# Modulation in three norms and on VectorE; one visit per step in two attentions

## The chip, the cores and the metric

One core of a Trainium2 chip runs the whole program. Its engines work side by side, each in its own fixed order: TensorE (PE, with its weight loads as PEld), VectorE (DVE), ScalarE (ACT), GpSimd (POOL) and SyncE (SP); transfers are issued from the queues of SP, ACT and POOL. They wait for one another by semaphores. The metric is the time of one execution on the device in microseconds (us), as the median of a few runs.

## The reference

The program is a stack for 512 latent tokens of width 1024. The first block has two layers with modulation: a vector per layer, from the condition `c` (and `c_ctx` for the 256 context tokens), gives shift, scale and gate of the mixer's norm and of the FFN's norm.

```python
mod = silu(c) @ ada_w[i] + ada_b[i]            # 6 x 1024 numbers per layer
sh1, s1, g1, sh2, s2, g2 = split(mod, 6)
h = rms_norm(x, norm1_g[i]) * (1 + s1) + sh1
x = x + g1 * mixer(h)                           # layer 0: gated linear attention, layer 1: neighbourhood attention
h = rms_norm(x, norm2_g[i]) * (1 + s2) + sh2
x = x + g2 * conv_ffn(h)
```

The second block has two layers, each with multi-head latent attention (causal softmax), stick-breaking attention and retention side by side, a gated output and an MLP. All is float32.

## The kernel before

Tokens stand along the free dimension, features along the partitions in `KD` = 8 groups of 128. A float32 product is made of three products of split operands: `mm3` (lines 327 to 334) multiplies high by high, low by high and high by low part; `weight()` (L311) loads a weight tile from SP's queue, ScalarE makes its high part (L319) and VectorE the low part (L320). In names, `hh` and `hl` (later `xh`, `xl`) are the halves of a normed input, `whi` and `wlo` those of a weight.

The modulation is cut into sections `sg` of 2048 numbers: section 0 for the first norm, then 1 to 5. Each section has two halves of 1024. There are two ways to work one out:

- `gada` on TensorE: 16 steps, a load of 128x1024 (tile `aw`) and two matmuls with `scT` (silu of the condition) as stationary operand, each into one of four groups of 32 columns of one bank (`ad`, L373); then VectorE transposes the bank (L380) and adds the bias. Sections 1 and 2 are worked out so during the GLA block, as filler; section 5 in the two norms around the first FFN, with loads on ScalarE's queue.
- `vada` on VectorE: per half, 16 loads of 128x512 (tile `at`, two buffers), each multiplied by two scalars and added to two sums (`aa`, L406 for the first, L408 for the others); then matmuls with a unit operand (L416) move the sums to the layout. Sections 3 and 4 are worked out so during the first FFN.

Filler is put in by `weave` (L229): a main generator yields how much time its step leaves to other engines, and the filler is advanced until it has yielded as much. `mixed` (L241) puts one step of a side generator into a filler whenever that has yielded `every`; in the GLA block `every` is `AEV` (2.5), and `ada()` (L803) is the side. The program's builder then sets each engine's order by when operands are ready, so an operation that depends on loads alone can stand far ahead of its place in the code; buffers of a pool keep it from running before they are free.

A norm goes in four steps: the squares' sums over the 8 groups (`sumsq`, L479, on VectorE), one product with ones on TensorE (`rstd`, L351), logarithm and exponential on ScalarE (L301), and `modulate`: VectorE (L498), ScalarE (L510, the high half) and VectorE again (L511, the low half). For the very first norm this is `modulate0`: ScalarE (L520), POOL (L521) and VectorE (L524). L576 applies the root there. "Norm 1" below is the one ahead of the first FFN, "norm 2" ahead of the neighbourhood attention, "norm 3" ahead of the second FFN. `block1_out` writes a block's output into the residual: L866 and L869 on VectorE.

The neighbourhood attention (`na`) runs `attend` for pairs of heads: scores of a step (L1004), transposes of the step two back (`trans`, L1027), and every other step the value products of the steps four back (`mix`, L1044), with a yield after each, so that the next heads' projection comes in between. `mla` in the second block does the same (scores, `mla_tr`, `mla_av`, L1426) with stick-breaking and retention as filler.

Of the kernel before, what the change touches and what calls it, by code (L numbers as in the profile page):

```python
# [17 lines left out]
P = 128  # L18
# [3 lines left out]
KD = 8  # L22
# [46 lines left out]
AEV = 2.5  # L69
# [78 lines left out]
def _lay_out(inp):  # L148
# [7 lines left out]
    for l in range(2):  # L156
        w = g["ada_w"][l].reshape(KD, P, 6, KD, 4, 32)
        b = g["ada_b"][l].reshape(6, KD, P)
        for va, vb in ((1, 0), (2, 3), (4, 5)):
# [4 lines left out]
            else:  # L164
                aw.append(s.transpose(0, 1, 4, 2, 3, 5).reshape(KD, P, 2048))
# [92 lines left out]
class Net:  # L258
# [127 lines left out]
    def vada(self, sg, pool):  # L386
        nc, io = self.nc, self.io
        m = self.mod[sg] = self.C.tile([P, 16, 2], F32, name=f"mod{sg}")
        b = self.vec("ada_b", 16 * sg, 16).unsqueeze(2).to_broadcast([P, 16, 2])
        steps = [(half, kc, c) for half in range(2) for kc in range(KD) for c in range(2)]  # L390

        def load(half, kc, c):
            t = self.sb(pool, [P, 512], "at", 2)
            o = 1024 * half + 512 * c
            nc.sync.dma_start(out=t, in_=io["ada_w"][sg - 1, kc, :, o:o + 512])
            return t

        t = load(*steps[0])
        for i, (half, kc, c) in enumerate(steps):
# [10 lines left out]
            yield  # L410
            if kc + c == KD:
                ps, R = self.mm(), slice(64 * half, 64 * half + 64)
# [5 lines left out]
                d = self.sb(pool, [P, NT], "acc", 1)[:, :512]  # L418
                nc.vector.transpose(out=d[R], in_=ps[R])
                nc.vector.tensor_tensor(out=m[R], in0=d[R].rearrange("p (j r) -> p j r", r=32)[:, :, 0:2], in1=b[R],  # L420
                                        op=ALU.add)
                yield
# [59 lines left out]
    def token_rstd(self, pool, x, parts, tags, ps=None):  # L482
# [68 lines left out]
    def gla(self, x, rs, hh, hl, yd, pool, early):  # L551
# [321 lines left out]
    def ffn(self, l, x, hh, hl, sg, pool, parts, tcv, tyh, tyl, side=iter(())):  # L873
# [4 lines left out]
        def proj(piece):  # L878
# [6 lines left out]
            next(side, None)  # L885
            next(side, None)
# [25 lines left out]
    def na(self, hh, hl, yh, yl, pool):  # L912
# [943 lines left out]
```

## Time and profile before

| | |
|---|---|
| median of three executions | 3698.85 us (3698.39 to 3700.05) |
| profiled execution | 3697.38 us, span 3695.6 us |
| PE busy | 3617.4 us, 98% of the span |
| VectorE busy | 2175.7 us, 59% |
| ScalarE busy | 1434.2 us, 39% |
| POOL busy | 361.7 us, 10% |
| mean TensorE clock granted | 0.994 |
| mean DMA rate | 97 GB/s |

A page of the profile names each group of instructions by line, engine and tile, with busy time, mean duration of one and the idle time before it. A busy PE isn't PE at its peak: records of matmuls overlap, and the time from one start to the next tells what one costs. Lines are those of the kernel before.

### The profile page before, as it was taken

The page shows a single profiled execution, that of the slowest core. Times are in us where ns is not written, and L with a number is a line of the kernel's source. Part 1 is how long each engine was busy: PE and PEld are TensorE (multiplying, and loading weights), DVE is VectorE, ACT ScalarE, POOL GpSimd, SP SyncE. Part 2 cuts the span into 40 slices and gives each one's busy share as a digit, 9 for nine tenths or more (in the row PEclk, how much of TensorE's full clock was granted, in tenths as well). Part 3 has the DMA queues.
Part 4 walks back from the last instruction along what each step waited for, and adds up shares of the span by engine and source line. Part 5 has one row for each costly group of instructions (what it writes and reads, how often), then busy time and mean ns, then how long its engine had stood idle before and what let it go on. Part 6 is the DMA issues. An engine that isn't in the chain of part 4 may idle for free.

```text
span 3695.6 us, 48674 instructions
## 1 busy us (share of the span) xinstructions
PE 3617.4 (98%) x19296; PEld 2972.7 (80%) x19296; DVE 2175.7 (59%) x3471; ACT 1434.2 (39%) x2199; POOL 361.7 (10%) x342
## 2 busy tenths in 40 slices
PE   7999999999999998999999999999999999999998
PEld 5778878888878886888787877888888787788888
DVE  5566776364355776444766775544456687644446
ACT  4334432121344454333546534422234653432223
POOL 2000000000001110000210121210121012121011
PEclk9999999999999999999999999999999999999999
DMA  6332343232112222323322232323332223233323
GB/s 254 123 95 66 120 151 107 71 117 83 60 62 58 52 57 66 99 95 99 116 82 87 92 102 80 120 97 97 97 119 82 91 89 104 81 120 98 97 94 118
DMA packets 128931, 360.21 MB, mean 97 GB/s; under 512 B 31664, under 2 KB 33968, under 8 KB 128704
## 3 DMA queue, kind: packets, MB, share of 16 engines
q1 hardware_dynamic: 97632, 321.70, 27.1%
q10 hardware_dynamic: 28928, 27.47, 2.6%
q0 software_dynamic: 2144, 7.93, 0.6%
q8 instruction: 152, 2.49, 0.3%
q14 instruction: 75, 0.61, 0.1%
HBM read 342.10 MB, written 8.65 MB: 95 GB/s over the span
## 4 chain that ended last, share of the span: by engine, by line
PE 45%; DVE 3%; issue 1%; ACT 1%; POOL 0%; DMA 0%; SPq 0%; DVEq 0%; POOLq 0%; ACTq 0%
PE mm L330 13%; PE mm L334 13%; PE mm L332 13%; PE yp L1335 1%; DVE wlo L320 1%; PE yp L1426 1%; PE mm L1238 1%; PE ma L1495 1%; PE mm L1240 0%; PE mm L1239 0%; PE ma L1414 0%; DMA tf<-s 0%; POOL ta L1483 0%; DVE ta L1478 0%; PE ma L1398 0%
## 5 line engine op out<-in xcount | busy, mean ns | idle before, releaser
L319 ACT ACTIVATE whi<-wst 128x1024 fp32r<-128x1024 f32 (+3 forms) x519 | 544.1, 1049 | 1335.8 <-PE mm L332 1113.5
L320 DVE TENSOR_TENSOR wlo<-wst,whi 128x1024 fp32r<-128x1024 f32 (+3 forms) x519 | 690.0, 1330 | 270.6 <-ACT whi L319 264.8
L330 PE MATMUL mm<-xh,whi 128*128 128x512 f32 x1664 | 664.4, 400 | 6.1 <-DVE ta L1124 3.0
L332 PE MATMUL mm<-xl,whi 128*128 128x512 f32 x1664 | 651.1, 391 | 1.6 <-DVE xl L1153 1.6
L334 PE MATMUL mm<-xh,wlo 128*128 128x512 f32 x1664 | 650.4, 391 | 0.0
L330 PE MATMUL mm<-ty,whi 128*128 128x512 f32 (+1 forms) x1008 | 381.1, 378 | 0.1
L334 PE MATMUL mm<-ty,wlo 128*128 128x512 f32 (+1 forms) x1008 | 378.9, 376 | 0.0
L330 PEld LDWEIGHTS mm<-xh,whi 128*128 128x128 f32 x1664 | 313.5, 188 | 79.7 <-issue 15.4
L334 PEld LDWEIGHTS mm<-xh,wlo 128*128 128x128 f32 x1664 | 313.0, 188 | 69.0 <-issue 2.1
L332 PEld LDWEIGHTS mm<-xl,whi 128*128 128x128 f32 x1664 | 313.6, 188 | 62.6 <-DVE xl L1153 2.0
L330 PE MATMUL mm<-hh,whi 128*128 128x256 f32 (+2 forms) x1176 | 339.6, 352 | 7.7 <-ACT hh L510 2.9
L332 PE MATMUL mm<-hl,whi 128*128 128x256 f32 (+2 forms) x1176 | 333.2, 347 | 0.7 <-DVE hl L524 0.4
L334 PE MATMUL mm<-hh,wlo 128*128 128x256 f32 (+2 forms) x1176 | 331.2, 345 | 1.7 <-DVE wlo L320 1.7
L332 PE MATMUL mm<-ta,whi 128*128 128x512 f32 (+1 forms) x752 | 279.1, 371 | 0.4 <-DVE ta L325 0.4
L330 PEld LDWEIGHTS mm<-hh,whi 128*128 128x128 f32 (+1 forms) x1176 | 189.2, 189 | 56.7 <-issue 21.0
L330 PEld LDWEIGHTS mm<-ty,whi 128*128 128x128 f32 x1008 | 189.7, 188 | 37.6 <-issue 4.2
L334 PEld LDWEIGHTS mm<-ty,wlo 128*128 128x128 f32 x1008 | 189.6, 188 | 37.0 <-issue 2.6
L334 PEld LDWEIGHTS mm<-hh,wlo 128*128 128x128 f32 (+1 forms) x1176 | 189.8, 188 | 31.1 <-DVE wlo L320 2.7
L332 PEld LDWEIGHTS mm<-hl,whi 128*128 128x128 f32 (+1 forms) x1176 | 189.0, 188 | 27.8 <-DVE hl L508 1.8
L332 PEld LDWEIGHTS mm<-ta,whi 128*128 128x128 f32 x752 | 141.7, 188 | 25.1 <-DVE ta L325 0.6
L1681 DVE TENSOR_TENSOR x<-x,mm 128x512 f32<-128x512 f32 x56 | 38.5, 687 | 172.1 <-PE mm L334 172.1
L869 DVE SCALAR_TENSOR_TENSOR x<-mm,mod,x 128x512 f32<-128x512 f32 x52 | 38.9, 749 | 164.7 <-PE mm L334 164.7
(427 smaller groups left out, 5920.4 us busy)
## 6 DMA issues: line engine op xcount, KB each, us to landing
wst<-w_in SPq DMA_DIRECT2D x100, 512.0 KB, 3.4
wst<-ffn_in SPq DMA_DIRECT2D x88, 512.0 KB, 3.4
wst<-w_dn SPq DMA_DIRECT2D x70, 512.0 KB, 3.4
wst<-w_up SPq DMA_DIRECT2D x64, 512.0 KB, 3.4
aw<-ada_w SPq DMA_DIRECT2D x40, 512.0 KB, 5.1
at<-ada_w SPq DMA_DIRECT2D x64, 256.0 KB, 3.2
wst<-w_v SPq DMA_DIRECT2D x32, 512.0 KB, 3.4
wst<-ffn_out SPq DMA_DIRECT2D x32, 448.0 KB, 3.3
```

The lines of the kernel that those rows point to most:

```text
L319: nc.scalar.activation(out=hi[:, :n], in_=st[:, :n], func=AF.Copy)
L320: nc.vector.tensor_tensor(out=lo[:, :n], in0=st[:, :n], in1=hi[:, :n].bitcast(F32), op=ALU.subtract)
L330: nc.tensor.matmul(o, whi, xh, start=first, stop=False)
L332: nc.tensor.matmul(o, whi, xl, start=False, stop=False)
L334: self.after = nc.tensor.matmul(o, wlo, xh, start=False, stop=last)
L869: nc.vector.scalar_tensor_tensor(out=x[:, n, a:b], in0=o[:, :b - a], scalar=gsc, in1=x[:, n, a:b], op0=ALU.mult, op1=ALU.add)
L1238: nc.tensor.matmul(o, a, wh[:, ws], start=(k == 0), stop=False)
L1335: nc.tensor.matmul(yp[64 * e:64 * e + 64, sb * P:], v[h // 4][:, sb, c:c + 64], a, start=(sb == 0), stop=True, skip_group_check=True)
L1426: nc.tensor.matmul(yp[64 * e:64 * e + 64, b * P:b * P + P], vm[p // 2][:, c, c0:c0 + 64], T[:, c * P:c * P + P], start=(c == 0), stop=(c = ...
L1495: nc.tensor.matmul(z[:, (s2 - s) * P:], wt, part, start=False, stop=True, skip_group_check=True)
L1681: nc.vector.tensor_tensor(out=x[:, n, :], in0=x[:, n, :], in1=o, op=ALU.add)
```

## The change

1. In the GLA block the side is now `vada` of the first half of section 2, then `gada(1)`; `gada(2)` is gone. `AEV` goes from 2.5 to 4.4.
2. `vada` takes a list of halves, loads on POOL's queue, ends each half with eight unit matmuls of 256 columns in four groups, and yields 0.
3. `gadah` is new: one half section on TensorE, with matmuls of 256 columns over the four groups. Norm 1 has (2, second half), norm 2 (5, first half), both in 8 steps of 1024 columns with seven `aw` buffers on ScalarE's queue; norm 3 has (5, second half) in 16 steps of 512 columns, with four buffers named `bm` on POOL's queue.
4. The sections from 2 on are laid out in memory by halves.
5. `attend` and `mla` issue value products, transposes and scores of a step in one go and then yield once.

```diff
-AEV = 2.5
+AEV = 4.4
@@ vada
-    def vada(self, sg, pool):
+    def vada(self, pool, parts, dst):
...
-            nc.sync.dma_start(out=t, in_=io["ada_w"][sg - 1, kc, :, o:o + 512])
+            nc.gpsimd.dma_start(out=t, in_=io["ada_w"][sg - 1, kc, :, o:o + 512])
...
-            yield
+            yield 0.0
...
+                ps = self.mm()[:, :256]
                 for r in range(2):
-                    for g in range(2):
-                        o = 64 * half + 32 * g
-                        nc.tensor.matmul(ps[o:o + 32, :], self.unit[:, r, :], acc[r][:, 512 * g:512 * g + 512],
+                    for g in range(4):
+                        nc.tensor.matmul(ps[32 * g:32 * g + 32, :], self.unit[:, r, :], acc[r][:, 256 * g:256 * g + 256],
...
+    def gadah(self, sg, v, width, lag, tile, queue, bank):
+        nc, io = self.nc, self.io
+        steps = [(kc, o) for kc in range(KD) for o in range(0, 1024, width)]
+        st = []
+        for i in range(len(steps) + lag):
+            if i < len(steps):
+                kc, o = steps[i]
+                t = tile()
+                queue.dma_start(out=t, in_=io["ada_w"][sg - 1, kc, :, 1024 * v + o:1024 * v + o + width])
+                st.append(t)
+            if i == lag - 1:
+                yield 0.0
+                ps = bank()[:, :256]
+            if i >= lag:
+                kc, o = steps[i - lag]
+                for c in range(0, width, 256):
+                    g = (o + c) // 256
+                    i2 = nc.tensor.matmul(ps[32 * g:32 * g + 32, :], self.scT[:, kc, :], st[i - lag][:, c:c + 256],
+                                          start=(kc == 0), stop=(kc == KD - 1), skip_group_check=True)
+                    self.order(i2, self.after)
+                yield 0.45
...
+        d = tile()[:, :256]
+        nc.vector.transpose(out=d, in_=ps)
...
@@ token_rstd
         acc = self.sumsq(pool, x, KD, parts, tags)
+        hook()
         rs = self.sb(tags.get("keep", pool), [P, hi], *tags["rs"])
@@ gla
         def ada():
-            for sg in range(1, 3):
-                yield from self.gada(sg, pool, (("aw", AW),), AW - 1)
+            yield from self.vada(pool, ((2, 0),), ("at", 2))
+            yield from self.gada(1, pool, (("aw", AW),), AW - 1)
@@ na
         def attend(p):
             for i in range(8 * p, 8 * p + 8):
-                scores(*steps[i])
-                yield 1.0
+                if i >= 4 and i % 2 == 0:
+                    mix(steps[i - 4][0] // 2, steps[i - 4][1])
                 if i >= 2:
                     trans(*steps[i - 2])
-                    yield 1.0
-                if i >= 4 and i % 2 == 0:
-                    mix(steps[i - 4][0] // 2, steps[i - 4][1])
-                    yield 2.0
+                scores(*steps[i])
+                yield 3.0
@@ mla
+                if i >= 4 and i % 2 == 0:
+                    mla_av(blocks[i - 4][0] // 2, blocks[i - 4][1])
+                if 0 <= i - 2 < n:
+                    mla_tr(*blocks[i - 2])
                 if i < n:
                     mla_scores(*blocks[i])
...
+                yield 3 * FILL[0]
@@ emit
-                ada = net.gada(5, F, (("aw", 7),), 7, nc.scalar)
+                ada = net.gadah(2, 1, 1024, 7, aw, nc.scalar, ad)
...
-                rs = norm(*ADA5[:2])
+                rs = norm(ada, *ADA5[:2])
+                drain(ada)
+                ada = net.gadah(5, 0, 1024, 7, aw, nc.scalar, ad)
+                next(ada)
...
-                        (None for sg in (3, 4) for _ in net.vada(sg, F)))
+                        net.vada(F, ((3, 0), (3, 1), (4, 0), (4, 1)), ("at", 2)))
...
+                    ada = net.gadah(5, 1, 512, 4, half, nc.gpsimd,
+                                    lambda: net.ps.tile([P, 512], F32, tag="sc", bufs=1, name="sc"))
+                    next(ada)
...
-                    rs = net.token_rstd(N, x2, [(0, NL)], dict(acc=("P", 3), rs=("rsb", 1), sq=("T", 4), keep=X))
+                    rs = net.token_rstd(N, x2, [(0, NL)], dict(acc=("P", 3), rs=("rsb", 1), sq=("T", 4), keep=X),
+                                        hook=lambda: [next(ada, None) for _ in range(6)])
+                    drain(ada)
```

The places where the order of instructions differs most, one engine at a time. Line numbers in the rows of after are those of the changed kernel, about 30 higher.

VectorE at the start of the program, before: the seven adds of the first norm's sum of squares (`A`), then the first piece of section 0 (`mod`, `gs`), and the application of the root to `F`.

```order
L1206 TENSOR_TENSOR fgm<-vecs 128x8
L479 TENSOR_TENSOR A<-A,gl 128x768 x7
L449 STREAM_TRANSPOSE gl<-ad 128x128
L453 TENSOR_TENSOR mod_167<-gl,vecs 128x2x4
L455 SCALAR_TENSOR_TENSOR gs_168<-mod_167,vecs 128x4
L576 TENSOR_TENSOR F<-F,bc 128x768
```

And after; the six rows left out repeat the pair of L509 and L407.

```order
L1235 TENSOR_TENSOR fgm<-vecs 128x8
L405 TENSOR_SCALAR aa<-at,scT 128x512 x4
L509 TENSOR_TENSOR A<-A,gl 128x768
L407 SCALAR_TENSOR_TENSOR aa<-at,scT,aa 128x512
...
L321 TENSOR_TENSOR wlo<-wst,whi 128x512
L479 STREAM_TRANSPOSE gl<-ad 128x128
L321 TENSOR_TENSOR wlo<-wst,whi 128x1024
L483 TENSOR_TENSOR mod_167<-gl,vecs 128x2x4
L407 SCALAR_TENSOR_TENSOR aa<-at,scT,aa 128x512
L485 SCALAR_TENSOR_TENSOR gs_168<-mod_167,vecs 128x4
```

Operations of `vada` (`aa`) stand ahead of the adds and between them, and on through the first projection.

POOL at the same place, before: its two loads of constants, then its share of the first modulation (`E`).

```order
L531 DMA cst<-con 128x261
L532 DMA vecs<-vecs 128x372
L521 ISA
L521 TENSOR_SCALAR E<-F,gs_168,mod_167 128x256
L521 TENSOR_SCALAR E<-F,gs_168,mod_167 128x512
```

And after; the rows of `E` that are left out are the same as before.

```order
L562 DMA cst<-con 128x261
L563 DMA vecs<-vecs 128x372
L394 DMA at<-ada_w 128x512 x8
L552 ISA
L552 TENSOR_SCALAR E<-F,gs_168,mod_167 128x256
...
L394 DMA at<-ada_w 128x512 x3
L552 TENSOR_SCALAR E<-y,gs_168,mod_167 128x256
```

Eight loads of `vada` stand ahead of the first `E`, and three, three and two behind its next groups.

TensorE around norm 3, before: the end of the output projection (`nyh`), the sum over the features (`mm` of `P`) and the second FFN's first products (`xh`).

```order
L330 MATMUL mm<-nyh,whi 128x512
L332 MATMUL mm<-nyl,whi 128x512
L334 MATMUL mm<-nyh,wlo 128x512
L351 MATMUL mm<-P,cst 128x512
L330 MATMUL mm<-xh,whi 128x512 x3
L332 MATMUL mm<-xl,whi 128x512
```

And after.

```order
L331 MATMUL mm<-nyh,whi 128x512
L333 MATMUL mm<-nyl,whi 128x512
L335 MATMUL mm<-nyh,wlo 128x512
L442 MATMUL sc<-bm,scT 32x256 x8
L352 MATMUL mm<-P,cst 128x512
L442 MATMUL sc<-bm,scT 32x256 x24
L331 MATMUL mm<-xh,whi 128x512 x3
L333 MATMUL mm<-xl,whi 128x512
```

The 32 matmuls of the half section stand around the sum, eight ahead of it and 24 behind it, ahead of the FFN.

VectorE there, before: the last residual update, the last add of squares (`P`), and the modulation (`ta`).

```order
L866 SCALAR_TENSOR_TENSOR x_3452<-mm,mod_5731,x_3452 128x8x16 x4
L320 TENSOR_TENSOR wlo<-wst,whi 128x1024
L479 TENSOR_TENSOR P<-P,T 128x512
L498 SCALAR_TENSOR_TENSOR ta<-x_3452,gs_12368,rsb 128x512 x3
L511 SCALAR_TENSOR_TENSOR xl<-ta,mod_5731,xh 128x512 x3
```

And after.

```order
L897 SCALAR_TENSOR_TENSOR x_3462<-mm,mod_6340,x_3462 128x8x16 x4
L321 TENSOR_TENSOR wlo<-wst,whi 128x1024
L509 TENSOR_TENSOR P<-P,T 128x512
L449 STREAM_TRANSPOSE bm<-sc 128x256
L451 TENSOR_TENSOR mod_8491<-bm,vecs 128x16
L529 SCALAR_TENSOR_TENSOR ta<-x_3462,gs_12498,rsb 128x512 x3
L542 SCALAR_TENSOR_TENSOR xl<-ta,mod_6340,xh 128x512 x3
```

The transpose of the half section's bank (`sc`) and its bias stand between the sum of squares and the modulation.

## Rows read from the trace of the kernel before

**Rows 1.** The page's busy times by engine.

```profile
PE 3617.4 (98%) x19296; PEld 2972.7 (80%) x19296; DVE 2175.7 (59%) x3471; ACT 1434.2 (39%) x2199; POOL 361.7 (10%) x342
```

**Rows 2.** Windows: length, busy (records), clock, DMA share, GB/s; first L373 alone.

```profile
61.00:250.00 189.00, 37.65 (x128) 5.05 (x128) 0.99 0.40 129
...
249.00:319.00 70.00, 69.93 (x498) 63.48 (x494) 49.27 (x67) 34.98 (x41) 2.89 (x2) 1.00 0.17 54
319.00:490.00 171.00, 164.84 (x1053) 144.44 (x1052) 120.32 (x163) 71.44 (x90) 3.00 (x2) 1.00 0.36 119
```

**Rows 3.** Timeline of PE: first hl product; first line after the projection.

```profile
27.47 0.90 PE L332 MATMUL mm<-hl,whi 128*64 128x512 f32 x2 [0.41 <-DVE hl L524]
...
60.64 0.28 PE L639 MATMUL mm<-whi,hh 128*128 128x256 f32 x1
```

**Rows 4.** Windows, all engines: PE, PEld, DVE, ACT, POOL, clock, DMA share.

```profile
25.00:46.00 21.00, 20.59 (x183) 14.37 (x182) 12.87 (x20) 6.72 (x10) 10.96 (x12) 0.79 1.02 400
46.00:61.00 15.00, 15.00 (x140) 12.26 (x140) 4.43 (x7) 5.03 (x9) 3.31 (x4) 1.00 0.14 50
1452.00:1460.00 8.00, 1.92 (x6) 0.69 (x5) 4.74 (x9) 4.05 (x6) 0.00 (x0) 0.81 0.23 73
```

**Rows 5.** Timeline at norm 3: PE, then DVE.

```profile
1455.60 1.10 PE L351 MATMUL mm<-P,cst 128*128 128x512 f32 x2 [3.04 <-DVE P L479]
1459.73 1.65 PE L330 MATMUL mm<-xh,whi 128*128 128x512 f32 x3 [3.04 <-ACT xh L510]
...
1458.11 2.08 DVE L498 SCALAR_TENSOR_TENSOR ta<-x,gs,rsb 128x512 f32<-128x512 f32 x3 [2.66 <-ACT rsb L301]
```

**Rows 6.** Timeline of PE: one filler step and what follows.

```profile
116.00 1.05 PE L373 MATMUL ad<-aw,scT 128*32 128x512 f32 x4
116.98 0.62 PE L330 MATMUL mm<-hh,whi 128*128 128x512 f32 x2
```

**Rows 7.** Timeline of PE at norm 1.

```profile
500.26 1.06 PE L373 MATMUL ad<-aw,scT 128*32 128x512 f32 x8 [3.91 <-issue]
...
512.18 1.01 PE L330 MATMUL mm<-hh,whi 128*128 128x512 f32 x2 [2.89 <-ACT hh L510]
```

**Rows 8.** DMA issues: tile, queue, count, size, median us to landing.

```profile
aw<-ada_w SPq DMA_DIRECT2D x40, 512.0 KB, 5.1
at<-ada_w SPq DMA_DIRECT2D x64, 256.0 KB, 3.2
...
xd<-x POOLq DMA_DIRECT2D x16, 256.0 KB, 2.3
...
vecs<-vecs POOLq DMA_DIRECT2D x1, 186.0 KB, 7.0
```

**Rows 9.** Timeline of PE: one cluster of unit products.

```profile
590.26 1.91 PE L416 MATMUL mm<-aa,unit 128*32 128x512 f32 x8
```

**Rows 10.** Groups of VectorE: busy, mean ns, idle before and its releaser.

```profile
L408 DVE SCALAR_TENSOR_TENSOR aa<-at,scT,aa 128x512 f32<-128x512 f32 x112 | 78.2, 747 | 28.2 <-DMA at<-ada_w 28.2
...
L406 DVE TENSOR_SCALAR aa<-at,scT 128x512 f32<-128x512 f32 x16 | 7.2, 474 | 10.5 <-PE mm L416 7.1 <-DMA at<-ada_w 3.3
```

**Rows 11.** Timeline of PE: two clusters of value products and what follows.

```profile
1182.28 1.09 PE L1044 MATMUL po<-T,v 128*64 128x128 f32 x16
1183.30 0.39 PE L968 MATMUL mm<-whi,hh 128*128 128x256 f32 x1
1183.53 0.28 PE L969 MATMUL mm<-wlo,hh 128*128 128x256 f32 x1
...
1224.24 0.65 PE L1044 MATMUL po<-T,v 128*64 128x128 f32 x6
1224.82 0.76 PE L1027 MATMUL tp<-cst,P 128*128 128x128 f32 x5
```

**Rows 12.** Timeline at the start: DVE, then POOL.

```profile
10.79 6.27 DVE L479 TENSOR_TENSOR A<-A,gl 128x768 f32<-128x768 f32 x6 [0.77 <-ACT gl L477]
...
22.90 5.62 POOL L521 TENSOR_SCALAR E<-F,gs,mod 128x256 f32<-128x256 f32 x4 [20.34 <-DVE F L576]
```

More of the change, by code (lines that the diff above doesn't have):

```diff
@@ L164, in _lay_out @@
             else:
-                aw.append(s.transpose(0, 1, 4, 2, 3, 5).reshape(KD, P, 2048))
+                s = s.transpose(0, 1, 2, 4, 3, 5) if len(aw) >= 1 else s.transpose(0, 1, 4, 2, 3, 5)
+                aw.append(s.reshape(KD, P, 2048))
             ab.append(np.concatenate([b[va], b[vb]], 0).T)
@@ L384, in gada, with load @@
         self.mod[sg] = m
-    def vada(self, sg, pool):
+    def vada(self, pool, parts, dst):
         nc, io = self.nc, self.io
[L388 to L392, printed above, removed]
+        steps = [(sg, v, kc, c) for sg, v in parts for kc in range(KD) for c in range(2)]
+        def load(sg, v, kc, c):
             t = self.sb(pool, [P, 512], "at", 2)
-            o = 1024 * half + 512 * c
-            nc.sync.dma_start(out=t, in_=io["ada_w"][sg - 1, kc, :, o:o + 512])
+            o = 1024 * v + 512 * c
+            nc.gpsimd.dma_start(out=t, in_=io["ada_w"][sg - 1, kc, :, o:o + 512])
             return t
         t = load(*steps[0])
-        for i, (half, kc, c) in enumerate(steps):
+        for i, (sg, v, kc, c) in enumerate(steps):
             ahead = load(*steps[i + 1]) if i + 1 < len(steps) else None
@@ L409, in vada @@
             t = ahead
-            yield
+            yield 0.0
             if kc + c == KD:
-                ps, R = self.mm(), slice(64 * half, 64 * half + 64)
+                if sg not in self.mod:
+                    self.mod[sg] = self.C.tile([P, 16, 2], F32, name=f"mod{sg}")
+                ps = self.mm()[:, :256]
                 for r in range(2):
-                    for g in range(2):
-                        o = 64 * half + 32 * g
-                        nc.tensor.matmul(ps[o:o + 32, :], self.unit[:, r, :], acc[r][:, 512 * g:512 * g + 512],
+                    for g in range(4):
+                        nc.tensor.matmul(ps[32 * g:32 * g + 32, :], self.unit[:, r, :], acc[r][:, 256 * g:256 * g + 256],
@@ L417, in vada @@
                                          start=(r == 0), stop=(r == 1), skip_group_check=True)
[L418 to L422, printed above, removed]
+                d = self.sb(pool, [P, 256], *dst)
+                nc.vector.transpose(out=d, in_=ps)
@@ new lines, in vada @@
+                b = self.vec("ada_b", 16 * sg + 8 * v, 8).unsqueeze(2).to_broadcast([P, 8, 2])
+                nc.vector.tensor_tensor(out=self.mod[sg][:, 8 * v:8 * v + 8, :], in1=b, op=ALU.add,
+                                        in0=d.rearrange("p (j r) -> p j r", r=32)[:, :, 0:2])
+                yield 0.0
[10 more added lines that the diff above has]
+            if i == lag - 1:
+                yield 0.0
+                ps = bank()[:, :256]
[7 more added lines that the diff above has]
+                yield 0.45
+        if sg not in self.mod:
+            self.mod[sg] = self.C.tile([P, 16, 2], F32, name=f"mod{sg}")
+        d = tile()[:, :256]
+        nc.vector.transpose(out=d, in_=ps)
+        b = self.vec("ada_b", 16 * sg + 8 * v, 8).unsqueeze(2).to_broadcast([P, 8, 2])
+        nc.vector.tensor_tensor(out=self.mod[sg][:, 8 * v:8 * v + 8, :], in1=b, op=ALU.add,
+                                in0=d.rearrange("p (j r) -> p j r", r=32)[:, :, 0:2])
@@ L480, in sumsq, with token_rstd @@
         return acc
-    def token_rstd(self, pool, x, parts, tags, ps=None):
+    def token_rstd(self, pool, x, parts, tags, ps=None, hook=lambda: None):
         lo, hi = min(p[0] for p in parts), max(p[1] for p in parts)
@@ L884, in proj @@
                          k == 0, k == KD - 1)
-            next(side, None)
-            next(side, None)
+            for _ in range(2):
+                next(side, None)
             return outs
@@ L1781, in emit @@
                 F = f.enter_context(pool("F0"))
-                ada = net.gada(5, F, (("aw", 7),), 7, nc.scalar)
+                aw = lambda: net.sb(F, [P, 1024], "aw", 7)
+                ad = lambda: net.ps.tile([P, 512], F32, tag="ad", bufs=1, name="ad")
+                ada = net.gadah(2, 1, 1024, 7, aw, nc.scalar, ad)
                 net.block1_out("gla_wo", KD, lambda k: hh[:, k, :], lambda k: hl[:, k, :], x, 1, 0, [LATP, CTXP],
@@ L1790, in emit, with norm @@
                 net.ps = f.enter_context(tc.tile_pool(name="psum2", bufs=1, space=PSUM))
-                def norm(before, after):
+                def norm(ada, before, after):
                     for _ in range(before):
@@ L1803, in emit @@
                 net.ffn(0, x, hh, hl, 2, F, [LATP, CTXP], ("cv", 3), ("yh", 9), ("yl", 9),
-                        (None for sg in (3, 4) for _ in net.vada(sg, F)))
+                        net.vada(F, ((3, 0), (3, 1), (4, 0), (4, 1)), ("at", 2)))
                 gs = net.gains(3, 0, "norm1_g", 1)
                 net.prefetch(*(net.io["na_qk"][i, 0] for i in (0, 8)))
-                rs = norm(*ADA5[2:])
+                rs = norm(ada, *ADA5[2:])
                 drain(ada)
```

8 lines of the change are left out of this document (1 added, 7 removed).

## The prediction

> **What bounds the kernel now.** I read the page first. TensorE (PE) is busy for 3617.4 us of the span and VectorE (DVE) for 2175.7 [rows 1]. So an edit pays where it takes work from PE, and costs where it makes PE wait; time on DVE, ScalarE and the queues counts only there. Next I asked for one line's busy time by stretch: L373, the modulation's matmuls, takes 37.65 us between 61 and 250 us, inside the GLA block, while the stretch 249 to 319, which has none of them, shows PE full all the same (69.93 of 70) [rows 2]. So they fill no hole: they are work on the bound engine. The timelines then gave the start and the norms. At the start PE's first hl product begins at 27.47 us and the first projection ends at 60.64, where the next line starts [rows 3]; in between PE is nearly dense (20.59 of 21 us, then 15 of 15, [rows 4]), so what delays the start delays the end. At norm 3 (after the neighbourhood attention, before the second FFN) PE waits 3.04 us, sums at 1455.60, waits 3.04 us again and starts the FFN at 1459.73 [rows 5].
>
> The durations come from the execution of 3697.38 us (span 3695.6, and 1.8 us around it), 1.47 us under the median 3698.85. The sum below is a difference, so I add it to the median.
>
> **The filler in the GLA block.** One step is two matmuls into two of four column groups, 0.98 us (116.00 to 116.98, [rows 6]), and the product behind it starts its successor 0.11 late, as behind a value product [rows 11]. The 32 steps cost 37.65 busy and some 3 for the exits, 40. In the order of after 16 of them are gone (half of that section goes to VectorE, half to norm 1), and the other 16 stand in nine clusters of 10, 3, 3, 1, 4, 7, 1, 1 and 2 matmuls. At norm 1 eight records that use all four groups take 1.06 us, as long as four records with two groups in the GLA block take [rows 6, 7]: the groups run beside each other, and a cluster costs its rounds of four matmuls. 3+1+1+1+1+2+1+1+1 = 12 rounds x 0.98 + 9 x 0.11 = 12.8; I take 14. Gain 26. Against it: the cluster of ten needs a fifth tile where there are four buffers, so that load starts only after the cluster's first step. SP's loads of this kind take 5.1 us [rows 8], of which the other steps cover some 1.5: a wait of 3.5. Net -22.5 (ends -26 and -17, if the cluster of seven waits as well).
>
> **Unit products of the VectorE form.** Four clusters of 1.91 us [rows 9] become five of half the columns over four groups, 0.98 each by the same reading: 4.9 for 7.6, about -2.5. In the FFN their loads move from SP's queue to POOL's. DVE waits 28.2 us for them today [rows 10] and PE doesn't notice, because DVE has the room. If POOL's queue were half as slow again, 14 us more would fall on DVE, still in its idle time: 0. Were DVE full there, those 14 would come on top.
>
> **The attentions.** In the neighbourhood attention 16 records of value products take 1.02 us (1182.28 to 1183.30) and 6 take 0.58 (1224.24 to 1224.82): 0.044 each and 0.32 per cluster; the product behind starts its successor after 0.23 instead of 0.12 [rows 11], an exit of 0.11. By the order there are 53 such clusters instead of 56, of which 33 instead of 12 are followed by transposes; in the two later layers it is 30 of 34 instead of none. No row shows an exit into transposes by itself, so between 0 and 0.11 is saved on each of 51; I take the middle, 0.05, hence 2.6, and 3 x 0.43 = 1.3 less a little filler that moves: -3.5 (0 to -7). Value product, transpose and score keep their distance of two steps each, so no wait of the chain between them is shortened or opened.
>
> **Norms 1 and 2.** Both keep eight steps, now of four quarter matmuls each. At norm 1 PE has 3.91 us idle ahead of the first steps and 2.89 ahead of the FFN, the latter for ScalarE's hh [rows 7], behind six loads that ScalarE issues. In after it issues one before the reciprocal root and seven behind the third hh: up to 2.9 comes back. But VectorE's loads now pass through POOL's queue, and DVE's share of the last residual stands behind the operations that wait for them: up to +3. I take -1. Norm 2: 0 (-1 to +1).
>
> **The start.** VectorE's half of section 2 waits for nothing but its loads, so its 32 operations stand first: four ahead of the sum of squares, one behind each of its adds but the last, 14 in all before the first hl, and all 32 within the first projection. They take 474 and 747 ns [rows 10]; six of the seven adds took 10.79 to 17.06 [rows 12]. There are two buffers; each load waits on POOL's queue until both operations on its buffer are done, while POOL's own share of the projection (from 22.90 on, [rows 12]) stands behind 8, 11 and 14 of the loads. I ran these orders against each other by hand with one time per load. At 2.3 us, as POOL's writes later show [rows 8], the adds end at about 22.5, the first hl product comes at 39 and the projection ends at 64.5: +4. At 3.2 (SP's loads of this size, [rows 8]): +5. At 5, a guess for a stretch in which transfers fill the DMA engines (1.02 up to 46 us, [rows 4]), the last hl comes at 69: +12. At 7.0, which vecs (186 KB, the same queue) took in the first 9 us [rows 8], at 80: +22. Contended loads up to 46 us and free ones after it (0.14, [rows 4]): +10.
>
> The Trainium skill ("DMA: Bandwidth & Descriptors", section on the anatomy of one DMA on the SWDGE path) gives a transfer of POOL's queue 2.0 us plus its bytes over 436 GB/s, an estimate of 2.6 for 256 KB, by which the start would cost 4 and the sum be 6 lower. The row of vecs [rows 8] says otherwise for a busy start. Another page, "SBUF — State Buffer" (section on the two separate sides), speaks against the move: a DVE operation in its two-port mode keeps POOL from writing descriptors. L406's 474 ns for as many columns as L408 has at 747 could be such a mode [rows 10]; four of them would hold the queue for 1.9 us. No run here shows it, and the sum leaves it out.
>
> **Norm 3.** Here 16 steps of two small matmuls are added: four before the sum of squares, twelve between it and the FFN's first product, and DVE transposes their result before it may modulate. The FFN doesn't need it yet; only the order holds it up. With four buffers, loads 5 to 16 come in three rounds, each load behind the step that frees its buffer. Taking 2.9 us per load (between POOL's 2.3 and SP's 3.2, [rows 8]) and the issues one behind the other: four steps end by 1453.6; the next four tiles are asked for by 1455 and land by 1457.9; the third round lands from 1460 to 1462, the last from 1463.4 to 1465.2; transpose and bias take 0.7. DVE's modulate starts at about 1466.3 instead of 1458.11 [rows 5], and the FFN follows as before: +8.2. At 2.3 it is +6.8, at 5 it is +14. PE's clock was 0.81 in this stretch [rows 4], and a longer hole may stretch the low level a little: +8.5.
>
> **Sum.** -22.5 - 2.5 - 3.5 - 1 + 0 + 10 + 8.5 = -11.0, and 3698.85 - 11.0 = 3687.9 us.
>
> **Rivals.**
> 1. Slow landing on POOL's queue. At 7.0 us, the row of vecs, the start costs 22 and norm 3's three rounds 20: -11 + 12 + 11.5 = +12.5, 3711 us. It breaks even near 5.8 us per load. For it: vecs took that on the same queue [rows 8]. Against it: that was in the first 9 us; later writes took 2.3, and at norm 3 the DMA share was 0.23 [rows 4]. Chance 0.12.
> 2. Quick landing (2.3 to 2.6), also of the fifth tile in the cluster of ten: start +4, norm 3 +7, filler -26, together -22, 3677 us. For it: POOL's later rows. Against it: DMA at 1.02 [rows 4]. Chance 0.18. The fit of the DMA page leads here.
> 3. The filler's time isn't free to take: where GLA's scan waits (319 to 490, PE 164.84 of 171, [rows 2]), matmuls taken out earlier turn into waits, because what they held apart follows sooner. Half of the 22.5 lost: 3699 us. For it: those 6.2 idle us. Against it: 249 to 319, full without any filler. Chance 0.18.
> The forecast as summed has 0.52, and 3679 to 3697 as its own range.
>
> **How the numbers follow.** A change under 0.2% (7.4 us) can't be told from none. The forecast lies 3.6 beyond that bound with an uncertainty of about 8: of its 0.52, 0.35 is faster, 0.16 same, 0.01 slower. Rival 2 is all faster, 0.18; rival 3 is 0.03 faster, 0.14 same, 0.01 slower; rival 1 is 0.04 same, 0.08 slower. Together 0.56, 0.34 and 0.10. The range runs from a little under rival 2's value to two thirds of the way to rival 1's: 3674 to 3704.
>
> **What would show it.** The modulation's matmuls with about 14 us in the GLA block and one wait for a load inside their first cluster; the first hl product near 40 us and the first projection's end at 68 to 72; DVE's transpose at norm 3 some 7 us after the sum's end, PE waiting for loads in between; value products followed at once by transposes, each attention 1 to 2 us shorter. I'm wrong if the first projection ends at 61 (the loads are hidden) or beyond 80, or if the time from there to norm 1 shrinks by less than 15 us.

## The result and the profile after: 22.7 us slower

The changed kernel takes 3722.11 us (median of 4 runs, 3718.46 to 3722.58) against 3699.45 of the kernel before on the same chip: a ratio on record of 1.0058, interval 1.0044 to 1.0072. One of the four executions of the kernel before took 10478.56 us; the other three took 3698.39 to 3700.05. The prediction said 3687.9 and a range of 3674 to 3704. The time lies above the range, on the other side of no change. The profiled execution took 3722.58 us, span 3720.8.

Span and busy times on the page:

```profile
span 3720.8 us, 49003 instructions
...
PE 3609.0 (97%) x19408; PEld 2984.7 (80%) x19408; DVE 2199.6 (59%) x3507; ACT 1439.5 (39%) x2199; POOL 417.4 (11%) x438
```

PE is busy for 8.4 us less than in [rows 1], and the span is 25.2 longer. So work was taken off the bound engine as meant, and some 34 us of waits came in its place. The same matmul looked up in both traces says where (after minus before):

| stretch | predicted | measured |
|---|---|---|
| start, to the end of the first projection | +10 | +17.5 (78.18 against 60.64) |
| from there to the last product ahead of norm 1 | -22.5 | -17.8 (495.56 against 495.82, less the 17.5) |
| norm 1, to the first FFN's first product | -1 | +3.2 |
| first FFN, unit products | -2.5 | about +3.5 |
| norm 2 and neighbourhood attention | part of -3.5 | about +0.6 |
| norm 3, to the second FFN's first products | +8.5 | +15.4 |
| the layers behind it | rest of -3.5 | about +2.6 |
| all, to the last matmul | -11.0 | +25.1 |

**The start.** DVE's timeline, after (start, us, engine, line, operation, [idle before <-releaser]):

```profile
12.47 0.95 DVE L509 TENSOR_TENSOR A<-A,gl 128x768 f32<-128x768 f32 x1
17.14 0.75 DVE L407 SCALAR_TENSOR_TENSOR aa<-at,scT,aa 128x512 f32<-128x512 f32 x1 [3.72 <-DMA at<-ada_w]
17.80 0.95 DVE L509 TENSOR_TENSOR A<-A,gl 128x768 f32<-128x768 f32 x1
...
25.35 0.75 DVE L407 SCALAR_TENSOR_TENSOR aa<-at,scT,aa 128x512 f32<-128x512 f32 x1 [2.00 <-DMA at<-ada_w]
...
27.55 0.95 DVE L509 TENSOR_TENSOR A<-A,gl 128x768 f32<-128x768 f32 x1
```

The adds (`A`) stand one behind each modulation operation (`aa`), and these wait for loads. The sum of squares ends at 28.5, where [rows 12] had 17.06. For the eight loads that are issued up to 36 us, the view of the tile `at` tells:

```profile
DMA to landing us min/median/max: 4.0/5.8/8.5
```

POOL's timeline there shows both sides of the queue, its loads and its share `E`:

```profile
32.21 0.54 POOL L394 DMA_DIRECT2D at<-ada_w  x1 [3.74 <-DVE aa L407]
33.92 14.12 POOL L552 TENSOR_SCALAR E<-F,gs,mod 128x256 f32<-128x256 f32 x8 [1.17 <-DVE F L607]
```

`E` begins at 33.92 instead of 22.90 [rows 12]. Its pieces also take longer: a median of 1847 ns for the first eight, against 984 before; no run asks why. PE follows:

```profile
28.55 2.93 PE L352 MATMUL mm<-A,cst 128*128 128x512 f32 x4 [6.35 <-DVE A L509]
...
44.10 0.79 PE L333 MATMUL mm<-hl,whi 128*64 128x512 f32 x2 [3.09 <-DVE hl L555]
...
78.18 0.28 PE L670 MATMUL mm<-whi,hh 128*128 128x256 f32 x1
```

The first hl product comes at 44.10 (before 27.47, [rows 3]). The windows of 25 to 46 and 46 to 61 us (PE, PEld, DVE, ACT, POOL, clock, DMA share, GB/s) answer to [rows 4]: PE has 12.86 of 21 us where it had 20.59, and the DMA engines, free again from 46 us on before (0.14), are still at 0.78.

```profile
25.00:46.00 21.00, 12.86 (x129) 8.31 (x130) 18.66 (x27) 8.64 (x14) 13.16 (x9) 0.88 0.95 344
46.00:61.00 15.00, 14.71 (x145) 11.52 (x145) 8.42 (x13) 2.52 (x4) 7.13 (x9) 0.94 0.78 288
```

**The GLA block.** Windows of L374, the old L373, alone (length, PE busy, PEld busy, clock, DMA share, GB/s), then PE's timeline at its first cluster:

```profile
76.00:250.00 174.00, 6.25 (x34) 1.11 (x34) 0.97 0.24 79
249.00:319.00 70.00, 4.23 (x22) 0.60 (x22) 1.00 0.20 65
319.00:490.00 171.00, 3.14 (x8) 0.42 (x8) 0.99 0.37 123
```

```profile
89.55 1.92 PE L374 MATMUL ad<-aw,scT 128*32 128x512 f32 x16
94.66 1.18 PE L374 MATMUL ad<-aw,scT 128*32 128x512 f32 x4 [3.19 <-DMA aw<-ada_w]
```

The 64 matmuls are busy for 13.6 us (14 predicted), and the wait for the fifth tile is there, 3.19 (3.5 predicted). Later in the block PE's timeline shows two more kinds of wait:

```profile
305.13 1.05 PE L374 MATMUL ad<-aw,scT 128*32 128x512 f32 x4 [0.80 <-DMA aw<-ada_w]
306.43 1.05 PE L374 MATMUL ad<-aw,scT 128*32 128x512 f32 x4 [0.24 <-DMA aw<-ada_w]
...
398.54 0.61 PE L335 MATMUL mm<-hh,wlo 128*128 128x512 f32 x2 [3.20 <-DVE wlo L321]
```

The cluster of seven matmuls waits for its loads as well, 1.04 us, and projection products wait 4.3 us for DVE's `wlo`, which stands behind operations of the scan there (0.4 before). In all, PE's waits in this block rise from 7.6 to 13.4 us.

**Norm 1.** PE, then DVE:

```profile
507.41 1.94 PE L442 MATMUL ad<-aw,scT 128*32 128x256 f32 x16 [11.35 <-issue]
509.28 2.83 PE L352 MATMUL mm<-acc,cst 128*128 128x512 f32 x4
...
515.13 0.61 PE L331 MATMUL mm<-hh,whi 128*128 128x512 f32 x2 [0.29 <-ACT hh L541]
```

```profile
500.21 2.74 DVE L407 SCALAR_TENSOR_TENSOR aa<-at,scT,aa 128x512 f32<-128x512 f32 x4
505.40 0.75 DVE L407 SCALAR_TENSOR_TENSOR aa<-at,scT,aa 128x512 f32<-128x512 f32 x1 [2.45 <-DMA at<-ada_w]
506.07 0.74 DVE L900 SCALAR_TENSOR_TENSOR x<-s,mod,x 128x512 f32<-128x512 f32 x1
```

The wait ahead of the FFN shrank from 2.89 [rows 7] to 0.29. But the last residual (L900) stands behind five operations of the next `vada` and their load, and PE waits 11.35 us ahead of its steps and the sum, instead of 3.91.

**Norm 3.** PE, POOL and DVE:

```profile
1459.58 1.07 PE L442 MATMUL sc<-bm,scT 128*32 128x256 f32 x16
1462.69 1.10 PE L352 MATMUL mm<-P,cst 128*128 128x512 f32 x2 [2.04 <-DVE P L509]
1464.65 1.65 PE L442 MATMUL sc<-bm,scT 128*32 128x256 f32 x8 [0.86 <-DMA bm<-ada_w]
...
1477.68 1.69 PE L442 MATMUL sc<-bm,scT 128*32 128x256 f32 x8 [1.10 <-DMA bm<-ada_w]
1482.24 1.65 PE L331 MATMUL mm<-xh,whi 128*128 128x512 f32 x3 [2.87 <-ACT xh L541]
```

```profile
1460.52 1.07 POOL L433 DMA_DIRECT2D bm<-ada_w  x2 [49.91 <-PE sc L442]
...
1466.03 1.12 POOL L433 DMA_DIRECT2D bm<-ada_w  x2 [3.16 <-PE sc L442]
```

```profile
1479.42 0.45 DVE L449 STREAM_TRANSPOSE bm<-sc 128x256 f32<-128x256 f32 x1 [16.87 <-PE sc L442]
1480.28 2.08 DVE L529 SCALAR_TENSOR_TENSOR ta<-x,gs,rsb 128x512 f32<-128x512 f32 x3 [0.20 <-DVE mod L451]
```

Loads go out in pairs, each pair behind the matmuls that free its buffers. A pair's round is load, two steps, load: 1460.52, then 1466.03, then 1471.07. DVE's modulation begins 17.6 us behind the start of the sum's matmul (1480.28 - 1462.69), before 2.51 [rows 5]. The view of the tile `bm` tells its loads, 256 KB each; the prediction had taken 2.9:

```profile
DMA to landing us min/median/max: 3.2/3.8/5.6
```

### The profile page after: what moved, and what is told of

Read it like the earlier page. It is cut to its first block, busy times and chain, and to the rows that moved or that the text cites. A ratio compares the mean times of both kernels' runs of the same rounds, so it can differ in the third digit from the quotient of the medians.

```text
span 3720.8 us, 49003 instructions
## 1 busy us (share of the span) xinstructions
PE 3609.0 (97%) x19408; PEld 2984.7 (80%) x19408; DVE 2199.6 (59%) x3507; ACT 1439.5 (39%) x2199; POOL 417.4 (11%) x438
## 3 DMA queue, kind: packets, MB, share of 16 engines
q10 hardware_dynamic: 28928, 27.47, 2.6%
q8 instruction: 153, 2.51, 0.3%
## 5 line engine op out<-in xcount | busy, mean ns | idle before, releaser
L331 PEld LDWEIGHTS mm<-xh,whi 128*128 128x128 f32 x1664 | 313.6, 189 | 78.2 <-issue 12.4
L331 PE MATMUL mm<-hh,whi 128*128 128x512 f32 (+2 forms) x1176 | 335.0, 348 | 6.2 <-ACT hh L551 2.7
L333 PE MATMUL mm<-hl,whi 128*128 128x512 f32 (+2 forms) x1176 | 333.9, 347 | 5.6 <-DVE hl L555 4.9
L335 PE MATMUL mm<-hh,wlo 128*128 128x512 f32 (+2 forms) x1176 | 331.6, 346 | 4.9 <-DVE wlo L321 4.9
L900 DVE SCALAR_TENSOR_TENSOR x<-mm,mod,x 128x512 f32<-128x512 f32 x52 | 39.0, 749 | 165.9 <-PE mm L335 165.9
```

The source lines that it names most:

```text
L331: nc.tensor.matmul(o, whi, xh, start=first, stop=False)
L333: nc.tensor.matmul(o, whi, xl, start=False, stop=False)
L335: self.after = nc.tensor.matmul(o, wlo, xh, start=False, stop=last)
L900: nc.vector.scalar_tensor_tensor(out=x[:, n, a:b], in0=o[:, :b - a], scalar=gsc, in1=x[:, n, a:b], op0=ALU.mult, op1=ALU.add)
```

## The experiments

They ran in three batches, each beside the kernel before (medians 3699.89, 3699.88 and 3699.55 us). Executions of one kernel differ by up to 12 us (norm3_resident: 3701.11 to 3713.18), and a trace shows one of them. So a stretch is known to a few us only: the GLA block takes 17.8 us less than before in the changed kernel, and 17.5, 15.5 and 14.3 less in three kernels below in which nothing up to norm 1 was edited (norm3_off, norm3_resident, norm1_guard; the builder's order differs a little among them). The first batch took the three places and the attentions apart.

**spread.** Loads of the first `vada` behind POOL's last `E`, and each of its operations behind DVE's preceding operation of the projection or the scan (an order only, no wait).

```diff
+                self.lastE = nc.gpsimd.tensor_scalar(out=u[:, a:b], in0=x[:, j, a:b],
...
+            i0 = nc.gpsimd.dma_start(out=t, in_=io["ada_w"][sg - 1, kc, :, o:o + 512])
+            self.order(i0, self.lastE)
...
+                    i1 = nc.vector.scalar_tensor_tensor(out=a, in0=t, scalar=sc, in1=a, ...)
+                self.order(i1, self.lastV)
```

> The changed kernel, with VectorE's half of section 2 kept at its place in the GLA block: its loads stand behind POOL's share of the first projection and each of its operations behind the VectorE work of the scan that precedes it in the code. Theory (the 32 operations at the start, and the loads they wait for, cost some 17 us): the first projection ends at 61 to 62 us instead of 78, and the time falls from 3722 to 3704-3708. Rival (the work costs as much wherever it stands, because the scan waits for VectorE too): 3718-3722, the time lost between 80 and 490 us.

3711.29 us (3705.56 to 3712.63), ratio 1.0029 [1.0016, 1.0041]: between what the theory and the rival expected. PE's timeline has the start back, with the first hl product at 26.59:

```profile
26.59 0.56 PE L333 MATMUL mm<-hl,whi 128*64 128x512 f32 x2 [1.47 <-DVE hl L557]
...
58.69 0.28 PE L672 MATMUL mm<-whi,hh 128*128 128x256 f32 x1
```

Just ahead of norm 1 it is 16.3 us ahead of before, where the changed kernel was 0.3 ahead: the start's loss is real and comes off by moving the side work alone. Only some 11 us of that reach the end; its norm 3 costs 15.6 as well, and in the profiled execution norm 1 loses 3.6, the first FFN 4.5 and the attention 6.0.

**loads_once.** 14 of the 16 loads of the first `vada` are left out; its operations read the two tiles that are there.

```diff
+            if sg == 2 and len(self.kept) == 2:
+                self.kept.reverse()
+                return self.kept[1]
```

> The changed kernel, but VectorE's half of section 2 loads two tiles and uses them over and over (14 of its 16 loads are left out, so this half section is not the one of the reference); all its operations stay at the start. Theory (at the start VectorE and POOL wait for loads that land after 5 to 6 us): the sum of squares ends near 23 us instead of 28.5, the first projection at 65 to 67 instead of 78, the time is 3709-3712. Rival (VectorE's own work at the start is what costs): projection's end at 74 or later, 3717-3722.

3711.93 us, ratio 1.0035 [1.0025, 1.0046]. The last add ends at 24.38 us (DVE's row) and the first projection at 69.39 (PE's), between the two, so neither theory has it alone:

```profile
23.43 0.95 DVE L515 TENSOR_TENSOR A<-A,gl 128x768 f32<-128x768 f32 x1
```

```profile
69.39 0.28 PE L676 MATMUL mm<-whi,hh 128*128 128x256 f32 x1
```

Of the 17.5 us the 14 loads make 8.8 (78.18 to 69.39). The other 8.7 are DVE's own operations ahead of the sum and of hl, with the two loads that are left, for which DVE waits 1.15 and 1.25 us.

**norm3_off.** (5, second half) on VectorE in the first FFN, the steps at norm 3 gone (the lines that go are not shown).

```diff
-                        net.vada(F, ((3, 0), (3, 1), (4, 0), (4, 1)), ("at", 2)))
+                        net.vada(F, ((3, 0), (3, 1), (4, 0), (4, 1), (5, 1)), ("at", 2)))
```

> The changed kernel with the second half of section 5 worked out on VectorE during the first FFN (a fifth half there) and no modulation at norm 3. Theory (norm 3 waits through three rounds of loads that land after 3.5 to 5.5 us): the time from the last output product to the second FFN's first product falls from 23 to 7.6 us, 3704-3708. Rival (a fifth half delays the first FFN, whose VectorE already waits 53 us for loads): 3714 or more, the first FFN 5 us longer or more.

3707.08 us (3701.82 to 3712.28), ratio 1.0020 [1.0010, 1.0029]: 15.0 below the changed kernel. Across norm 3 its shift against before does not change (13.1 us on both sides). So norm 3's loss belongs to the steps put there. The fifth half has a price of its own: the first FFN loses 5.6 us against before, 2 more than in the changed kernel.

**attn_only.** The kernel before with the new `attend` and `mla` alone.

```diff
...
+                if i >= 4 and i % 2 == 0:
+                    mix(steps[i - 4][0] // 2, steps[i - 4][1])
                 if i >= 2:
                     trans(*steps[i - 2])
-                    yield 1.0
...
+                scores(*steps[i])
+                yield 3.0
```

> The kernel before with the change to the two attentions alone. The prediction's reading (the exit from value products into a float32 product is saved where transposes follow): 3.5 us faster, 3695-3697. The reading from the trace after (the late start falls on the scores that come next instead, nothing is saved): 3698-3701, no difference above 0.1%; the score products next to the transposes take as much longer as the projection's products take less.

3697.34 us, ratio 0.9990 [0.9981, 0.9999]: -2.6 us, between -7 and -0.4, so the time cannot tell -3.5 from nearly nothing. The profiled execution shows 0.6 less. The changed kernel's timeline shows what happens to an exit:

```profile
1206.53 1.31 PE L1075 MATMUL po<-T,v 128*64 128x128 f32 x20
1207.77 0.66 PE L1058 MATMUL tp<-cst,P 128*128 128x128 f32 x4
1208.19 0.36 PE L1035 MATMUL sl<-k,q 128*128 128x256 f32 x1
1208.39 0.28 PE L1036 MATMUL sl<-kz,q 128*128 128x256 f32 x1
```

In the kernel before:

```profile
1176.68 0.60 PE L1027 MATMUL tp<-cst,P 128*128 128x128 f32 x4
1177.04 0.36 PE L968 MATMUL mm<-whi,hh 128*128 128x256 f32 x1
1177.24 0.28 PE L969 MATMUL mm<-wlo,hh 128*128 128x256 f32 x1
```

Behind the value products, four transposes take 0.42 us to the next start; behind a projection product they take 0.36. What follows the transposes takes 0.20 to its successor where the next one takes 0.12, in both kernels: a projection product before, a score now. So of the exit of 0.11 behind value products [rows 11] 0.06 is left in the transposes, and the 0.08 behind transposes has only changed its place. That is the 0.05 for each cluster that the prediction took. But summed over the neighbourhood attention by line, transposes and projection products give back 8.4 us (3.3, 2.9 and 2.2), and four of the score and value lines take 8.9 more (4.1, 1.85, 1.84 and 1.1). So a gain per exit is seen, and a gain of the stretch is not, in this trace.

The second batch put these together.

**norm1_guard.** In the changed kernel the FFN's `vada` operations are ordered behind norm 1's modulation on DVE.

```diff
+                    self.lastV = nc.vector.scalar_tensor_tensor(out=l, in0=u, scalar=bias, ...)
...
+                self.order(i1, self.lastV)
```

> The changed kernel, with VectorE's operations for sections 3 and 4 held behind the modulation of norm 1. Theory (at norm 1 the last residual update of VectorE stands behind five of these operations and their loads, 7 us later than before): PE's wait ahead of its first steps there falls from 11.4 to about 4 us, norm 1 ends 6 to 7 us earlier, 3715-3717. Rival (the wait is ScalarE's or the loads' of norm 1 itself): the wait stays above 9 us, 3720-3723.

3712.81 us (3704.80 to 3715.28), ratio 1.0028 [1.0015, 1.0041], 9.3 below the changed kernel and below the 3715 to 3717 expected. PE's first wait there is 1.42 us instead of 11.35, and norm 1 goes from +3 to -8: the half section there is a gain of its own, which the residual's place behind the loads had hidden.

**three_undone.** spread, norm3_off and norm1_guard together.

> The changed kernel with the start, norm 1 and norm 3 mended together: VectorE's half of section 2 spread over the GLA block, its operations for the first FFN behind norm 1's modulation, and the second half of section 5 in the first FFN too. Theory (the three waits are the loss, the rest of the change a gain of 20 in GLA, less 5 in the FFN for PE's slower pace): the three savings add up, 3687-3692, faster than the kernel before by 8 to 12. Rival (what is taken away at one wait is met at the next, as VectorE is the engine behind all of them): 3700-3706.

3679.40 us (3677.88 to 3683.85), ratio 0.9949 [0.9932, 0.9966]: it beats the kernel before by 20 us and the changed one by 43. That is more than the 35 by which the three alone add up (10.8, 15.0 and 9.3), and than was expected; where the other 8 come from is open. Norm 1 on PE:

```profile
479.10 1.07 PE L444 MATMUL ad<-aw,scT 128*32 128x256 f32 x16 [1.39 <-issue]
...
485.68 0.62 PE L331 MATMUL mm<-hh,whi 128*128 128x512 f32 x2 [0.44 <-ACT hh L543]
```

The 11.35 us are 1.39. It stands 18.6 us ahead of before just before norm 1, 26.5 behind it, and 21.6 ahead of norm 3. What the change takes from PE, with this half section on VectorE too, is worth about 20 us; the three waits cost 43.

**no_attention.** three_undone with the attentions as before (the diff of attn_only backwards).

> As three_undone, with the two attentions as in the kernel before. If the new order of the attentions costs 1 to 3 us (the trace after shows +1.4 in the neighbourhood attention and +1.8 in the later layers): 1 to 3 us faster than three_undone, 3685-3690. If it is worth the 3.5 us of the prediction: 3 to 4 slower than three_undone.

3683.27 us (3677.29 to 3686.83), ratio 0.9954 [0.9939, 0.9969]. That is 3.9 above three_undone, where 1 to 3 below it was expected. The intervals overlap nearly whole, so again the attentions can't be told from nothing; but both comparisons of medians (2.6 and 3.9) lie on the side of the prediction.

Three kernels are left, on sizes. **norm3_resident**: the changed kernel, with norm 3's first four loads used for all 16 steps (twelve loads left out).

```diff
+                if width == 512 and i >= 4:
+                    t = st[i - 4]
+                else:
+                    t = tile()
```

> The changed kernel, with four loads at norm 3 in place of 16: all 16 steps use these four tiles again (so this half section is not the one of the reference), the matmuls and the transpose stay. Theory (the loss at norm 3 is the three rounds of loads): from the last output product to the second FFN's first product 9 to 12 us instead of 23, the time 3709-3712. Rival (the matmuls and the transpose ahead of the modulation cost it, wherever the data come from): 17 us or more there, 3716-3722.

3705.56 us (3701.11 to 3713.18), ratio 1.0013 [1.0002, 1.0024]. PE at norm 3:

```profile
1462.03 1.50 PE L445 MATMUL sc<-bm,scT 128*32 128x256 f32 x24
1465.15 1.10 PE L352 MATMUL mm<-P,cst 128*128 128x512 f32 x2 [1.61 <-DVE P L512]
1466.17 2.37 PE L445 MATMUL sc<-bm,scT 128*32 128x256 f32 x40
1471.04 0.98 PE L331 MATMUL mm<-xh,whi 128*128 128x512 f32 x3 [2.50 <-ACT xh L544]
```

All 64 records take 3.9 us, mostly where PE waited before, and norm 3 costs 1.8 us more than before instead of 15.4; the time is below the 3709 to 3712 expected. So the rounds of loads are the loss, neither the matmuls nor their place. The granted clock is 1.00 from 1462 to 1480 us here, so what the low clock cost behind the waits is part of that loss; it was not separated.

**unit_swap** and **unit_tail** asked why the first FFN lost time though its clusters got shorter (1.00 us to the next product instead of some 1.84). Windows of 40 us without a cluster, in the FFN: before at 604 and at 744, then after at 604. attn_only, whose FFN is that of before, has 233 matmuls at 604 like it.

```profile
604.00:644.00 40.00, 40.00 (x233) 34.98 (x232) 29.78 (x43) 11.88 (x15) 0.00 (x0) 1.00 0.47 145
744.00:784.00 40.00, 40.00 (x229) 34.72 (x228) 27.84 (x41) 12.91 (x16) 0.00 (x0) 1.00 0.47 143
```

```profile
604.00:644.00 40.00, 40.00 (x228) 34.67 (x227) 33.03 (x48) 10.62 (x13) 6.48 (x12) 1.00 0.49 150
```

PE is full and at clock 1.00 in all, with 228 to 233 matmuls done. Six products (three of 512 columns, three of 256) take either 1.040 or 1.060 us, and a pace holds for whole stretches. Before has 1.060 only between its clusters at 725 and 933 us; the changed kernel has it from its first cluster, at 593 us, on, which costs about 5.3 us of the FFN. A cluster is not the only place where the pace turns: three_undone goes from 1.060 to 1.040 at 821.5 us, where PE waits 1.17 us for an operand, and back at its next cluster; the changed kernel waits 1.31 there, at 850 us, and stays at 1.060. Nor does the slower pace belong to the change: at the end of the GLA block six products take 1.06 us before (479.22 to 480.28) and 1.04 after (479.26 to 480.30). unit_swap is no_attention with the unit matmuls ordered by group first; unit_tail is three_undone with a product of 64 columns behind each cluster.

```diff
-                for r in range(2):
-                    for g in range(4):
+                for g in range(4):
+                    for r in range(2):
```

> As no_attention, with the eight unit matmuls of a half in another order (both rows of one column group after each other). It asks about PE's two paces in the first FFN (six matmuls in 1.04 or 1.06 us, constant from one unit cluster to the next). If the pace is set by how the cluster ends: the stretches between clusters change pace, and the FFN changes by 2 us or more in either direction. If the pace belongs to the place in the program: the same paces as in no_attention within 0.005 us per six.

3685.28 us, ratio 0.9960 [0.9945, 0.9975].

```diff
+                nc.tensor.matmul(full[0:32, 256:256 + 64], self.unit[:, 0, :], acc[0][:, 0:64], start=True, stop=True,
+                                 skip_group_check=True)
```

> As three_undone, with one more small product (64 columns, into unused columns of the same bank) behind each cluster of unit products. If PE's pace in the first FFN is set by the moment at which the products resume: some of the six stretches between clusters run at 1.040 us per six instead of 1.060, the FFN is 1 to 5 us shorter, 3674-3680. If not: all stretches at 1.060, and the time 0 to 1 us longer than three_undone.

3681.51 us, ratio 0.9949 [0.9930, 0.9968]. In both the pace of the FFN is 1.060 in every stretch. For unit_swap that is as in no_attention; unit_tail has lost the stretch at 1.040 that three_undone has from 821.5 to 908 us (228 matmuls against 233 from 830 to 870 us). What sets the pace is open.

## Why the prediction was wrong

**The start: mechanism right, size wrong.** The prediction had `vada` between the adds, POOL's `E` behind its loads, and PE late by both; all of it is there, but 17.5 us stand for 10. The step that failed is the hand run of the two orders, in two terms. Its floor was too low: at 2.3 us a load it gave +4, the adds ending at 22.5 and the projection at 64.5; loads_once, with 14 of 16 loads gone, still gives +8.7, with 24.4 and 69.4, and the two loads that are left explain at most 2.4 of it. And its contended load, 5 us by guess, was short: the first eight landed in 4.0 to 8.5 us, seven of them in 5.6 or more, with a median of 5.8. The free loads behind 46 us were taken nearly rightly, though the DMA engines stayed at 0.78 up to 61 us: those issued at 50 and 51 us took 5.1 and 4.7, the six behind them 3.2 to 3.8. Rival 1 is the closest of the cases, with +22 for the start and 3711 us in all. But its load of 7.0 was met by the first two alone (8.5 and 7.6), and at norm 3, where it had slow loads too, the median was 3.8.

By the estimate from the Trainium skill ("DMA: Bandwidth & Descriptors", anatomy of one DMA on the SWDGE path) a 256 KB load would take 2.6 us; no load of this size on POOL's queue landed in less than 3.2 here. The measurement decides: that figure holds in no stretch that mattered here.

**Norm 3: the round was mis-sized.** The three rounds are there, but one lasts about 5.3 us (1460.52 to 1471.07 is two), not 2.9 and its issue: 3.8 median for a load, then two steps of the pair, and these take longer than they do at full clock (1.65 for eight records where sixteen had taken 1.07; the granted clock is 0.59 between 1460 and 1483 us). 15.4 for 8.5. By the prediction's own scale, 6.8 at 2.3 us a load and 14 at 5, a load of 3.8 makes some 10.8, an estimate; the other 4 to 5 us are the steps between the loads, which its rounds hardly count. norm3_resident shows the rounds to be the loss: without the twelve loads 1.8.

**Norm 1: the wrong sign.** The step that failed is the wait put at up to +3. It was written for DVE's share of the residual behind the waiting operations, and netted against 2.9 given back. The sum is +3, but its parts are -8 (norm1_guard, whose waits are 1.42 for 3.91 and 0.44 for 2.89) and +11. The prediction did not walk through the five `vada` operations and their loads that stand ahead of L900, and its 2.9 given back counted only the second of these waits.

**The GLA block: right in kind, 4.7 us short.** 13.6 us busy, a wait of 3.2, net -17.8 for -22.5. PE's waits rise by 5.8 us, where 3.5 were foreseen. The sum left out the loads of the cluster of seven (1.04), which the prediction named as the lower end, and had nothing for PE waiting for DVE's `wlo`: 1.60 at 80 us, late with the start, and 4.3 around 400 us (0.4 before). The last is rival 3's mechanism at another place: what the filler had held apart follows sooner, but the scan's own products wait less than before (3.3 us against 5.7). These are read from the timelines and were not tried by themselves.

**Unit products: the term right, the stretch not.** Four clusters give 3.3 us less (-2.5 forecast); the slower pace takes 5.3, and one wait at 850 us some 2. No row of before had been read for a pace.

**The attentions: not decided.** 0.05 per cluster is what the rows show. The trace of the changed kernel has no gain in these stretches (+0.6 and +2.6), and lines of the scores and values take back what the exits give. The two comparisons of medians, 2.6 and 3.9 us, fit the -3.5; the first is only just clear of the noise, the second is not.

Of the signs by which it would show itself wrong, "the time from there to norm 1 shrinks by less than 15" and "beyond 80" did not come true: 17.8 and 78.2. They did not watch norm 1, and norm 3 had none but "some 7 us".

## What to carry to other kernels

Side work on an engine with idle time costs nothing only if the program's chain on that engine does not stand behind it: look in the order at what follows each operation that waits for a load, and let it begin behind the chain. A load's price is read from a stretch with the traffic that it will meet, and few buffers turn it into rounds of load plus the step that frees the buffer. Work moved to a wait of the bound engine is nearly free there if its operands have landed (3.9 us of matmuls for 1.8 in norm3_resident), and otherwise it makes the wait longer.

## What the runs showed of the hardware

- In the changed kernel, loads of 256 KB on POOL's queue landed in a median of 3.4 to 3.6 us in the first FFN (DMA share 0.31 to 0.33 there), never in less than 3.2, and in 4.0 to 8.5 at the start, with the DMA engines at 0.88 to 1.04 from 10 to 46 us. The `aw` loads of 512 KB on SP's queue took 8.5 median between 9 and 80 us, and 6.2 over the whole program.
- PE ran the same six products at 1.040 or 1.060 us, at clock 1.00 and without a wait, for whole stretches. The pace turned at clusters of short matmuls and, in three_undone, at a wait of 1.17 us; no run shows what sets it.
- Transposes straight behind value products take 0.06 us longer than behind a projection product, where a projection product straight behind value products starts its successor 0.11 late; and whatever follows transposes, score or projection product, starts its successor 0.08 late.
